# Values of the dilated heads: projected from neighbouring tokens, put in strided order through DRAM

## The chip, the cores and the metric

The kernel runs on one core of one Trainium2 chip. The metric is the device time of one execution in microseconds; lower is better. A core has TensorE (PE, with its weight loads shown apart as PEld), VectorE (DVE), ScalarE (ACT), GpSimd (POOL) and SyncE (SP), whose queue issues most of the DMAs here. Each engine works through its own instructions in program order.

## What is computed

Two layers of a hybrid decoder, for 512 prompt tokens and 64 sample tokens (8 sequences of 8) with shared weights. Only the attention of the prompt matters for this change:

```python
h = rmsnorm(x, norm1)
q, k, v, u, ga, gb = jnp.split(h @ w_in, ...)        # 12 heads of 64, in three groups of four
for g, (w, d) in enumerate(((128, 1), (512, 4), (2048, 16))):
    idx = q_idx[:, None] - jnp.arange(w // d + 1)[None, :] * d     # keys at distance 0, d, 2d, ...
    o[g], lse[g] = softmax attention of q over k[idx], v[idx]
o = sum over g of softmax(lse)[g] * o[g]
```

Queries of the two dilated groups meet only keys and values whose token number is the same modulo 4 (or 16). The keys and values are also outputs, in token order: the cache buffers of each group.

## The kernel before

Activations lie with the 1024 features on partitions: `h[k]` is one of eight tiles of 128 features by 576 tokens, split in a rounded part and a remainder (`h[k][:, 0]`, `h[k][:, 1]`). Weights stream in pieces of 512 KB (`raw`, two buffers, issued on SP's queue); ACT rounds each into `wh`, DVE subtracts to get `wl`, and each product is three matmuls (rounded by rounded, remainder by rounded, rounded by remainder).

A layer begins with nine units of the query, key and value projection: `UNITS = ("d", "a", "b", "e", "c")` for head pair p = 0, and the same without e for p = 1. Unit d makes query and key of group 0, a the queries and b the keys of groups 1 and 2, e the values of group 0 (both pairs), c the values of groups 1 and 2. In `qkv` (L450) a unit has two halves of one weight piece each; a half runs over four feature tiles k and four blocks j of 128 tokens, and each (k, j) is three matmuls of line L464 whose stationary operand is a 128 by 128 piece of `h[k]` and whose moving operand is 256 columns of weights, into the PSUM tile `mmq`. After each half eight matmuls of L476 do the sample tokens (`psd`). In all units but c, block j is the 128 neighbouring tokens 128j to 128j+127. In unit c, block j is every fourth token starting with j:

```python
def cls(v, r):
    return v[:, r:NP:4]
```

so that the values come out of the projection in the order in which the dilated heads use them.

`unit_out` (L482) takes a unit out of PSUM: four ACT operations multiply by the reciprocal root mean square of each token, a column of `rn` for each block. `stats` (L283) makes those columns: four for blocks of neighbouring tokens, one for the sample tokens, and four more (L292) for the blocks of every fourth token, which only unit c uses. It runs once a layer inside the first unit. For units d, a and b there follow a rotation on DVE (`rope`), transposes on PE (`trq`, L523) and the tiles `Td`, `Ta`, `Tb`; for c, the tile `vc`. Keys and values are written out by DMAs on SP's queue (L539 to L547).

`prompt(p)` (L549) is the attention of a head pair: scores (`sp`, L569 and L572), masks and maxima on DVE, exponentials on ACT, a mixing of the groups' weights by two small groups of matmuls (`ex`, L601 and L623), then `O`: eight steps, each of which scales a tile `P` on DVE (L639, L641), transposes it on PE (`trx`, L648) and multiplies by `ve` and `vc` (L661, L665). `decode(p, qb)` is the attention of the sample tokens over the caches: POOL multiplies cache pieces `kc` with the queries `qb` (`prod`), DVE sums the products (`SC<-prod`), later PE forms the outputs (`po`). The cache pieces and `qb` are DMAs on SP's queue; `qb` is itself spread through DRAM (`DQ`, `DR`).

The order of everything beside the main loops is fixed when the program is built, by a planner with a clock of its own, `now`. A main loop calls `tick(cost)` after each group (1.28 for the 12 matmuls of one k in `qkv`, whatever the unit; 0.72 for the six of one k in `gemm`). Side tasks are generators that sleep for some time, until an event (`mark`, with a delay `lat`), or until the planner's idea of an engine's end (`after`); whichever is due at a tick issues its next instructions there. `until` lets the planner's clock run on without main work. So planned times decide the order in each engine's queue, and the chip decides the rest. `prompt(p)` waits for the event `("V", "c", p)` just before it sets up `O`.

After the nine units come four groups of `u`, 16 gates with their products, `wo` and the feed-forward part, all `gemm` (L222, matmuls at L228). `until("S", 1)`, `until("ob", 0, l)` and `until("D", 1)` tie them to the attention.

The functions that the diff touches:

Of the kernel before, what the change touches and what calls it, by code (L numbers as in the profile page):

```python
# [7 lines left out]
F32 = mybir.dt.float32  # L8
F32R = mybir.dt.float32r
BF16 = mybir.dt.bfloat16  # L10
AF = mybir.ActivationFunctionType
# [26 lines left out]
def hybrid_decoder_kernel(ctx: ExitStack, tc: tile.TileContext, a, o):  # L38
    nc = tc.nc
    T, V, S, G, Q = nc.tensor, nc.vector, nc.scalar, nc.gpsimd, nc.sync  # L40
# [10 lines left out]
    drp = ctx.enter_context(tc.tile_pool(name="dr", bufs=1, space=DRAM))  # L51
# [15 lines left out]
    ident, ones, mask = C("ident"), C("ones"), C("mask")  # L67
# [90 lines left out]
    def mark(*key, lat=0.0):  # L158
        ev[key] = now[0] + lat
# [49 lines left out]
    V = Lane(V, 0.07, 960.0)  # L209
    S = Lane(S, 0.19, 1400.0)  # L210
    G = Lane(G, 0.1, 460.0)

    def post(delay, fn):
        def g():
            fn()
            return
            yield
        side(g(), delay)
# [49 lines left out]
    def cls(v, r):  # L268
        return v[:, r:NP:4]
# [11 lines left out]
        V.tensor_mul(r, r, q)  # L281

    def stats(sqs, full, key):  # L283
        n = 9 if full else 5
        ps = spp.tile([128, 512], F32, tag="s", name="st")
        for b in range(4):
            T.matmul(ps[:, b:b + 1], sqs[:, 128 * b:128 * b + 128], ones[:, 0:1], start=True, stop=True)
        for i in range(2):
            T.matmul(ps[64 * i:64 * i + 64, 4:5], sqs[:, NP:NT], ones[:, 0:1], start=True, stop=True)
        if full:  # L290
            for r in range(4):
                T.matmul(ps[:, 5 + r:6 + r], cls(sqs, r), ones[:, 0:1], start=True, stop=True)  # L292
        spend(0.2 * n)
        rs = tp.tile([128, 4, 9], F32, tag="rs", name="rs", bufs=2)
        rsqrt(rs, ps, n)
        r = rs[:, 2, :n]
        rb = tp.tile([128, NT], F32, tag="rb", name="rb", bufs=1)
        scale_of[key] = (rs[:, 2], rb)
        if full:
            mark("R", key, lat=max(V.t - now[0], 0.0) + 1.0)  # L300
        dgt = tp.tile([128, NT], F32, tag="t", name="dg")
        for b in range(5):
            m = 128 if b < 4 else 64
            dg = dgt[:, 128 * b:128 * b + m]
            V.tensor_scalar(out=dg[:m, :m], in0=ident[:m, :m], scalar1=r[:m, b:b + 1], scalar2=None, op0=ALU.mult)
        yield after(V, S, lag=1.6)
        ps2 = trp.tile([128, 512], F32, tag="tr", name="rps")
        for b in range(5):
            m = 128 if b < 4 else 64
            dst = ps2[:, 128 * b:128 * b + 128] if b < 4 else ps[:, 64:128]  # L310
            T.matmul(dst, ones[:m, :], dgt[:m, 128 * b:128 * b + m], start=True, stop=True)
        spend(1.0)
        S.copy(rb[:, 0:512], ps2)
        S.copy(rb[:, 512:576], ps[:, 64:128])
        if not full:
            mark("R", key)
# [41 lines left out]
    h, sqs = None, None  # L358
    for l in range(L):
# [90 lines left out]
        def qkv(p, unit):  # L450
            psm = mmp.tile([128, 4, 256], F32, tag="mm", name="mmq")
            psd = None
            for half in range(2):
                w = wnext()
                for kk in range(4):
                    k = 4 * half + kk
                    hi, lo = (w[i][:, 256 * kk:256 * kk + 256] for i in range(2))
                    for j in range(4):
                        if unit != "c":
                            xh, xl = (h[k][:, i, 128 * j:128 * j + 128] for i in range(2))  # L460
                        else:
                            xh, xl = (cls(h[k][:, i], j) for i in range(2))
                        for i, (x, ww) in enumerate(((xh, hi), (xl, hi), (xh, lo))):
                            T.matmul(psm[:, j], x, ww, start=(k == 0 and i == 0 and j % 2 == 0),  # L464
                                     stop=(k == 7 and i == 2 and j % 2 == 1), skip_group_check=True)
                    tick(1.28)
                if psd is None:
                    if (p, unit) != (0, "d"):
                        until("psd")
                        del ev[("psd",)]  # L470
                    psd = pdp.tile([128, 512], F32, tag="d", name="psd")
                for kk in range(4):
                    k = 4 * half + kk
                    hi, lo = (w[i][:, 256 * kk:256 * kk + 256] for i in range(2))
                    for i, ww in enumerate((hi, lo)):
                        T.matmul(psd[:, 0:256], hd[:, k], ww,  # L476
                                 start=(k == 0 and i == 0), stop=(k == 7 and i == 1))
                tick(0.85)
            side(unit_out(p, unit, psm, psd), ("R", ("a", l)))
            tick()  # L480

        def unit_out(p, unit, psm, psd):  # L482
            rn = scale_of["a", l][0]
            if unit == "e":
                nat = ve
            elif unit == "c":
                nat = pp.tile([128, 4, 256], F32, tag="vc", name="vc", bufs=1)
            else:
                nat = qp.tile([128, 4, 256], F32, tag="nat", name="nat", bufs=2)
            col = 0 if unit != "c" else 5  # L490
            for j in range(4):
                S.activation(nat[:, j], psm[:, j], AF.Copy, scale=rn[:, col + j:col + j + 1])
            dt = tp.tile([64, 256], F32, tag="t", name="dt")
            S.activation(dt, psd[64:128, 0:256], AF.Copy, scale=rn[64:128, 4:5])
            if unit == "d":
                dns[p] = dp.tile([64, 9, 128], F32, tag="dn", name="dn", bufs=1)
            DN = dns[p]

            def dsum(dst, c0, c1):
                src = psd[0:64, c0:c1]  # L500
                t = dt[:, c0:c1]
                if c1 - c0 == 256:
                    src, t = v3(src, 2), v3(t, 2)
                V.scalar_tensor_tensor(out=dst, in0=src, scalar=rn[0:64, 4:5], in1=t, op0=ALU.mult, op1=ALU.add)

            yield after(S)
            if unit == "e":
                dsum(DN[:, 6], 0, 128)
                dsum(ve1, 128, 256)
            else:  # L510
                dsum({"d": DN[:, 0:6:3], "a": DN[:, 1:3], "b": DN[:, 4:6], "c": DN[:, 7:9]}[unit], 0, 256)
            mark("psd")
            f0 = 128 * p
            if unit in "dab":
                if unit == "b":
                    side(decode_q(p, DN), 0.6)
                rope(nat.rearrange("p n (h d) -> p n h d", h=4), *rope_t, 128, 4, 4)
                yield after(V)
                tt = qp.tile([128, 2, 512], F32, tag="T" + unit, name="T" + unit, bufs=1)
                for i in range(2):  # L520
                    pt = trp.tile([128, 512], F32, tag="tr", name="trq")
                    for j in range(4):
                        T.transpose(pt[:, 128 * j:128 * j + 128], nat[:, j, 128 * i:128 * i + 128], ident)  # L523
                    spend(0.43)
                    dst = tt[:, i]
                    if unit != "d":
                        dst = dst.rearrange("p (r n) -> p n r", r=4)
                        pt = pt.rearrange("p (n r) -> p n r", r=4)
                    S.activation(dst, pt, AF.Copy, scale=0.125 if unit == "a" or (unit == "d" and i == 0) else 1.0)
                    yield 1.1  # L530
                tts[p][unit] = tt
                mark("T", unit, p, lat=0.3)
            else:
                if unit == "c":
                    vcs[p] = nat
                    side(decode_new(p, DN), 0.5)
                mark("V", unit, p, lat=0.3)
            if unit == "d":
                Q.dma_start(o["p128"][l, :, 0, f0:f0 + 128], nat[:, 3, 128:256])  # L539
            elif unit == "e":  # L540
                Q.dma_start(o["p128"][l, :, 1, :], nat[:, 3, :])
            elif unit in "bc":
                s = 0 if unit == "b" else 1
                order = "(b p) s f -> p b s f" if s == 0 else "(p b) s f -> p b s f"
                for i, n in enumerate(("512", "2048")):
                    Q.dma_start(o["p" + n][l].rearrange(order, b=4)[:, :, s, f0:f0 + 128],
                                nat[:, :, 128 * i:128 * i + 128])  # L547

        def prompt(p):  # L549
# [632 lines left out]
        h = hn  # L1182
# [127 lines left out]
```

## Time and profile before

| what | us |
|---|---|
| median of 3 runs | 1780.98 |
| the runs | 1780.54, 1780.98, 1784.67 |
| span of the profiled execution, first to last instruction | 1781.5 |
| PE busy in it | 1711.1 |
| DVE busy | 947.6 |
| ACT busy | 554.3 |
| POOL busy | 442.8 |

The profiled execution is told by its span; nothing else of its time is shown. The span stands 0.5 us above the median of the runs, so times read in the trace can be set against the median as they are. Layer 0 begins at 0 and layer 1 at about 884 us.

### The profile page before, as it was taken

How to read it: one execution, taken by the hardware profiler on the slowest of the kernel's cores; microseconds unless marked ns; L12 is line 12 of the kernel's file. 1: busy time of each engine (PE TensorE's matmuls, PEld its weight loads, DVE VectorE, ACT ScalarE, POOL GpSimd, SP SyncE). 2: the span in 40 equal slices, each digit the busy share in tenths (PEclk: the TensorE clock that was granted, in tenths of full speed). 3: DMA queues.
4: the chain of work that ended last, by engine and by line, in shares of the span. 5: the costliest groups of instructions: out<-in, count | busy, mean ns of one | idle time of the engine just before them, and what ended most of it. 6: DMA issues, size and time to landing. Idle time of an engine off the chain costs nothing. (4 is left out here: it accounts for less than half of the span.)

```text
span 1781.5 us, 30883 instructions
## 1 busy us (share of the span) xinstructions
PE 1711.1 (96%) x13008; PEld 1667.6 (94%) x13008; DVE 947.6 (53%) x1365; ACT 554.3 (31%) x882; POOL 442.8 (25%) x461
## 2 busy tenths in 40 slices
PE   8988999999999999999999799989999999999996
PEld 7978988989999999999999698888999999999996
DVE  6388679735544333343535977894454443434332
ACT  4423332223333222231334233311333331322232
POOL 2065128311111211211102622572111112121201
PEclk8999999999999999999999999999999999999998
DMA  4451653434244445443326326435243544444421
GB/s 157 156 164 62 197 155 116 130 105 144 99 166 165 173 156 175 153 176 117 120 89 202 105 97 209 134 99 168 68 158 120 173 168 165 156 174 155 172 84 54
DMA packets 137316, 251.04 MB, mean 141 GB/s; under 512 B 9532, under 2 KB 98108, under 8 KB 134346
## 3 DMA queue, kind: packets, MB, share of 16 engines
q1 hardware_dynamic: 132810, 194.27, 33.7%
q0 software_dynamic: 3648, 53.98, 8.4%
q8 instruction: 103, 1.69, 0.4%
q10 hardware_dynamic: 720, 0.82, 0.1%
q14 instruction: 35, 0.29, 0.1%
HBM read 237.30 MB, written 72.77 MB: 174 GB/s over the span
## 5 line engine op out<-in xcount | busy, mean ns | idle before, releaser
L228 PE MATMUL mm<-a,wh 128*128 128x256 f32 (+1 forms) x2304 | 413.2, 302 | 14.5 <-DVE mB L203 8.7
L203 DVE TENSOR_TENSOR wl<-raw,wh 128x1024 fp32r<-128x1024 f32 (+2 forms) x248 | 340.9, 1375 | 113.3 <-ACT wh L203 103.6
L228 PEld LDWEIGHTS mm<-a,wh 128*128 128x128 f32 x2304 | 350.5, 193 | 22.5 <-issue 21.5
L203 ACT CAST wh<-raw 128x1024 fp32r<-128x1024 f32 (+2 forms) x248 | 241.5, 974 | 403.7 <-PE mm L228 324.1
L228 PE MATMUL mm<-h,wh 128*128 128x256 f32 (+1 forms) x2048 | 354.8, 295 | 0.0
L228 PEld LDWEIGHTS mm<-h,wh 128*128 128x128 f32 x2048 | 306.2, 188 | 0.2
L203 POOL TENSOR_TENSOR prod<-kc,qb 128x1024 f32<-128x1024 f32 (+1 forms) x96 | 212.4, 2239 | 244.6 <-DMA kc<-in_c 191.8
L464 PE MATMUL mmq<-wh,a 128*128 128x256 f32 x1152 | 256.7, 318 | 3.1 <-DVE a L203 2.4
L228 PE MATMUL mm<-a,wl 128*128 128x256 f32 (+1 forms) x1152 | 249.4, 298 | 0.0
L464 PEld LDWEIGHTS mmq<-wh,a 128*128 128x128 f32 x1152 | 217.4, 228 | 6.3 <-DVE a L203 3.1
L228 PE MATMUL mm<-h,wl 128*128 128x256 f32 (+1 forms) x1024 | 218.0, 295 | 0.0
L203 POOL COPY pace<-beat 1x1 f32<-1x1 f32 x112 | 67.7, 605 | 544.9 <-DVE beat L203 544.9
L228 PE MATMUL mm<-m,wh 128*128 128x256 f32 (+1 forms) x1152 | 200.0, 295 | 0.0
L228 PEld LDWEIGHTS mm<-a,wl 128*128 128x128 f32 x1152 | 196.8, 192 | 0.0
L203 DVE TENSOR_TENSOR xr<-xr,mm 128x576 f32<-128x576 f32 (+2 forms) x88 | 61.6, 700 | 245.4 <-PE mm L228 221.9
L464 PE MATMUL mmq<-wl,a 128*128 128x256 f32 x576 | 181.0, 314 | 0.0
L228 PEld LDWEIGHTS mm<-m,wh 128*128 128x128 f32 x1152 | 173.3, 187 | 0.0
L228 PEld LDWEIGHTS mm<-h,wl 128*128 128x128 f32 x1024 | 171.4, 188 | 0.0
L464 PEld LDWEIGHTS mmq<-wl,a 128*128 128x128 f32 x576 | 131.4, 228 | 0.0
L203 ACT ACTIVATE zz<-z 128x576 f32<-128x576 f32 x64 | 43.9, 686 | 259.7 <-DVE z L203 259.7
L228 PE MATMUL mm<-m,wl 128*128 128x256 f32 x576 | 123.3, 295 | 0.0
L203 DVE SCALAR_TENSOR_TENSOR z<-mm,rb 128x576 f32<-128x576 f32 x64 | 48.5, 758 | 134.6 <-PE mm L228 128.0
(214 smaller groups left out, 1909.8 us busy)
## 6 DMA issues: line engine op xcount, KB each, us to landing
raw<-in_wup SPq DMA_DIRECT2D x64, 512.0 KB
raw<-in_wd SPq DMA_DIRECT2D x64, 512.0 KB
out_s<-in_c POOLq DMA_DIRECT2D x64, 508.0 KB, 3.9
kc<-in_c SPq DMA_DIRECT2D x40, 512.0 KB
raw<-in_wq SPq DMA_DIRECT2D x35, 512.0 KB
kc<-in_c SPq DMA_DIRECT2D x64, 256.0 KB
out_s<-in_c POOLq DMA_DIRECT2D x32, 504.0 KB, 4.8
raw<-in_wgb SPq DMA_DIRECT2D x16, 512.0 KB
```

Source lines behind the costliest of these rows:

```text
L203: return op(*args, **kw)
L228: T.matmul(ps[:, c0:c0 + t1 - t0], w, act[:, x, t0:t1], start=(i == 0 and j == 0), stop=(i == n - 1 and j == 2))
L464: T.matmul(psm[:, j], x, ww, start=(k == 0 and i == 0 and j % 2 == 0), stop=(k == 7 and i == 2 and j % 2 == 1), skip_group_check=True)
```

## The change

Unit c is projected like the other units, from blocks of 128 neighbouring tokens, with the columns of `rn` that the others use; the four extra columns of `stats` are gone. Its result goes to a tile `nat` (of the two buffers that d, a and b use in turn) and not to `vc`. From there a DMA writes it to a DRAM buffer `DV` in token order, and a second DMA reads `vc` from it so that block r holds every fourth token. Both are issued on SP's queue at planned times, 1.2 and 4.0 after the ACT operations. The event `("V", "c", p)` comes 9.0 after them on the planner's clock; it was 0.3 after the sums of the sample tokens. The cache outputs of unit c are now written from `nat` with the same row order as those of unit b.

```diff
     def stats(sqs, full, key):
-        n = 9 if full else 5
+        n = 5
...
-        if full:
-            for r in range(4):
-                T.matmul(ps[:, 5 + r:6 + r], cls(sqs, r), ones[:, 0:1], start=True, stop=True)
         spend(0.2 * n)
...
                     for j in range(4):
-                        if unit != "c":
-                            xh, xl = (h[k][:, i, 128 * j:128 * j + 128] for i in range(2))
-                        else:
-                            xh, xl = (cls(h[k][:, i], j) for i in range(2))
+                        xh, xl = (h[k][:, i, 128 * j:128 * j + 128] for i in range(2))
...
-            elif unit == "c":
-                nat = pp.tile([128, 4, 256], F32, tag="vc", name="vc", bufs=1)
             else:
                 nat = qp.tile([128, 4, 256], F32, tag="nat", name="nat", bufs=2)
-            col = 0 if unit != "c" else 5
             for j in range(4):
-                S.activation(nat[:, j], psm[:, j], AF.Copy, scale=rn[:, col + j:col + j + 1])
+                S.activation(nat[:, j], psm[:, j], AF.Copy, scale=rn[:, j:j + 1])
+            if unit == "c":
+                DV = drp.tile([512, 256], F32, tag=f"dv{l}{p}", name="DV")
+                vc = pp.tile([128, 4, 256], F32, tag="vc", name="vc", bufs=1)
+                vcs[p] = vc
+                post(1.2, lambda: Q.dma_start(DV.rearrange("(j p) f -> p j f", j=4), nat))
+                post(4.0, lambda: Q.dma_start(vc, DV.rearrange("(n r) f -> n r f", r=4)))
+                mark("V", unit, p, lat=9.0)
...
                 if unit == "c":
-                    vcs[p] = nat
                     side(decode_new(p, DN), 0.5)
-                mark("V", unit, p, lat=0.3)
+                else:
+                    mark("V", unit, p, lat=0.3)
...
-                order = "(b p) s f -> p b s f" if s == 0 else "(p b) s f -> p b s f"
                 for i, n in enumerate(("512", "2048")):
-                    Q.dma_start(o["p" + n][l].rearrange(order, b=4)[:, :, s, f0:f0 + 128],
+                    Q.dma_start(o["p" + n][l].rearrange("(b p) s f -> p b s f", b=4)[:, :, s, f0:f0 + 128],
                                 nat[:, :, 128 * i:128 * i + 128])
```

## Rows read from the trace of the kernel before

**Rows 1.** The page, part 1: busy us, share of the span, instructions.

```profile
PE 1711.1 (96%) x13008; PEld 1667.6 (94%) x13008; DVE 947.6 (53%) x1365; ACT 554.3 (31%) x882; POOL 442.8 (25%) x461
```

**Rows 2.** Busy us by stage: stretch, length, PE PEld DVE ACT POOL, clock, DMA, GB/s.

```profile
79.30:105.40 26.10, 26.10 (x132) 25.44 (x129) 15.56 (x20) 9.70 (x31) 9.83 (x5) 1.00 0.80 251
105.40:170.00 64.60, 50.41 (x416) 46.69 (x416) 61.33 (x67) 19.27 (x34) 42.99 (x19) 0.97 0.28 88
176.20:204.00 27.80, 27.80 (x150) 27.25 (x149) 12.19 (x26) 9.39 (x22) 0.00 (x0) 1.00 0.60 190
206.00:254.00 48.00, 46.76 (x457) 39.32 (x456) 37.48 (x83) 16.93 (x47) 11.17 (x22) 1.00 0.57 175
254.00:322.00 68.00, 60.19 (x429) 58.52 (x426) 62.85 (x61) 18.36 (x31) 53.41 (x24) 0.95 0.38 110
...
979.20:1042.00 62.80, 50.37 (x405) 46.73 (x405) 57.86 (x66) 17.71 (x33) 43.28 (x20) 0.95 0.30 94
```

**Rows 3.** The chain that ended last, layer 1: start, us, what.

```profile
1044.75 4.31 PE mmq L464 x36
...
1050.02 11.20 PE mmq L464 x48
...
1361.14 349.96 PE mm L228 x2634
```

**Rows 4.** PEld groups in 79.3 to 105.4, unit c: busy us, mean ns.

```profile
L464 PEld LDWEIGHTS mmq<-wh,a 128*128 128x128 f32 x64 | 17.9, 328 | 0.2
```

**Rows 5.** PEld groups in 57.5 to 69.0, units b and e.

```profile
L464 PEld LDWEIGHTS mmq<-wh,a 128*128 128x128 f32 x56 | 8.7, 190 | 0.0
```

**Rows 6.** Timeline of PE inside `stats`, layer 0: start, us, instruction.

```profile
31.21 0.95 PE L287 MATMUL st<-const,sqs 128*128 128x1 f32 x8
...
32.30 2.03 PE L292 MATMUL st<-const,sqs 128*128 128x1 f32 x8
```

**Rows 7.** Busy us behind `stats`, layer 0, columns as in the second group.

```profile
33.00:40.00 7.00, 7.00 (x41) 6.81 (x41) 3.73 (x16) 2.53 (x7) 0.00 (x0) 0.76 0.07 28
```

**Rows 8.** PE's waits in 105.4 to 170: us in total, times, longest.

```profile
PE trx L648 <- DVE P L203: 7.3, 7, 1.6
PE trq L523 <- DVE nat L203: 4.9, 2, 3.5
PE ex L623 <- DVE xt L203: 2.0, 1, 2.0
```

**Rows 9.** Groups in 105.4 to 170: busy us, mean ns, idle before.

```profile
L203 POOL TENSOR_TENSOR prod<-kc,qb 128x1024 f32<-128x1024 f32 (+1 forms) x19 | 43.0, 2284 | 18.8 <-DVE SC L203 15.7 <-DVE cc L203 3.1
...
L203 DVE TENSOR_REDUCE SC<-prod 128x16 f32<-128x1024 f32 (+1 forms) x22 | 21.7, 1013 | 0.0
L203 DVE TENSOR_SCALAR P<-P,cc 128x256 f32<-128x256 f32 (+1 forms) x16 | 18.6, 1199 | 0.0
```

**Rows 10.** DVE groups in 226 to 249, the same step of p = 1.

```profile
L203 DVE TENSOR_SCALAR P<-P,cc 128x256 f32<-128x256 f32 (+1 forms) x16 | 4.7, 343 | 0.0
```

**Rows 11.** Timeline of POOL: the first products of `decode(0)`.

```profile
92.48 6.09 POOL L203 TENSOR_TENSOR prod<-kc,qb 128x1024 f32<-128x1024 f32 x3 [75.47 <-DMA kc<-in_c]
100.87 3.77 POOL L203 TENSOR_TENSOR prod<-kc,qb 128x512 f32<-128x512 f32 x2 [2.29 <-DMA kc<-in_c]
```

**Rows 12.** Timeline of DVE at the end of unit c, p = 0.

```profile
106.40 0.17 DVE L203 COPY ct<-ex 128x16 f32<-128x16 f32 x1 [4.28 <-PE ex L601]
```

**Rows 13.** Timeline of PE: `O` set up, then its first use of `vc`.

```profile
113.40 0.38 PE L632 MATMUL O<-zero 1*128 1x512 bf16 x1
...
122.34 0.61 PE L665 MATMUL O<-PT,vc 128*64 128x128 f32 x8
```

**Rows 14.** Waits of SP's queue, whole span: us in total, times, longest.

```profile
SPq L111 <- DVE wl L203: 1201.2, 235, 12.3
...
SPq L695 <- DMA DR<-DQ: 17.8, 2, 9.0
...
SPq L707 <- DMA DS<-dn: 10.5, 4, 4.1
```

**Rows 15.** Waits of all engines: what the pooling mixer's tiles waited for.

```profile
POOL u L203 <- DMA out_p<-vc: 45.2, 1, 45.2
```

## The prediction

> **What bounds the kernel now.** I read the page first: PE is busy 96% of the span, the next engine 53% [rows 1]. So PE's own work sets the time, unless a stage says otherwise. Then I cut the first layer into stages [rows 2]. In the stretch 79.30 to 105.40, which is unit c of p = 0, PE is never idle. In the next, 105.40 to 170.00, PE is idle 14.2 us (64.60 less 50.41) and DVE is busy 61.33: this stage is DVE's. Unit c of p = 1 (176.20 to 204.00) is again all PE, 206 to 254 nearly so (1.2 idle), and 254 to 322 is DVE's once more (62.85 of 68). Layer 1 repeats it; its row for the first of DVE's stages has 12.4 idle. After the attention one unbroken run of PE matmuls of 350 us is on the chain that ended last [rows 3], so a gain that has reached that point lasts to the end. What is to be seen: PE time saved in unit c is worth its full size only where PE sets the next handover. The p = 1 unit leads into PE's stage, the p = 0 unit into one of DVE's.
>
> **The projection in unit c.** The chain holds the last 36 matmuls before unit c and 48 of unit c in one piece each [rows 3]: 4.31/36 = 0.1197 us against 11.20/48 = 0.2333 us, with the same operand sizes. The weight loads tell where it goes: 328 ns each in unit c [rows 4], 190 ns in the units before it [rows 5], at the full clock. The one thing that differs is the fourfold step of the loaded columns. Unit c has 96 matmuls of L464, so it saves 96 x 0.1136 = 10.9 us; two pairs and two layers make 43.6.
>
> **The statistics.** The four strided columns are eight matmuls that took 2.03 us where the eight unstrided ones took 0.95 [rows 6]. They begin 1.9 us before the next work does, so 1.9 goes per layer, 3.8 in all. That the step alone doubles a load shows here in another kind of matmul. Behind them, in layer 0, the granted clock was 0.76 over 7 us [rows 7]: about half of it at 1.2 instead of 2.4 GHz, worth 7 x 0.24 = 1.7 us. A shorter run of one-column matmuls may keep the clock up; I take 0, with 0 to 1.7 for the range. On the other side more PE idle in DVE's stage may lower it there: its rows stand at 0.97 and 0.95 already, and 0.03 of 64.6 is 1.9 per layer for one more fall; I take 0 here too.
>
> So PE has 47.4 us less to do. How much arrives?
>
> **p = 0, into DVE's stage.** PE reaches the first group of mixing matmuls (`ex`, end of unit c) at 79.3 - 1.9 + 26.1 - 10.9 = 92.6 instead of 105.4. Before, DVE sat 4.28 us until 106.40 for it [rows 12]. But POOL's first product started at 92.48, after its cache piece had landed [rows 11], and that piece hangs on unit b, which moves by 1.9 alone: 90.6. The sum of the first product stands on DVE ahead of what `ex` needs, so `ex` can't run before about 90.6 + 2.3 + 1.0 + 0.6 = 94.5. Two of the 12.8 us are lost at once. Then DVE has only sums to do until `O` is set up: POOL feeds a product each 2.28 us, a sum takes 1.01 [rows 9]. `O` is now held by the planner for 9.0 of its units after unit c; at 1.28 for a k that PE does in 12 x 0.12 = 1.44 us, with 0.85 and 0.8 of other work and the wait of 2.0 that `ex` had before [rows 8], about 12.4 us behind unit c's end at 96.6: 109. It stood at 113.40 [rows 13], so the eight scaling steps, which with the sums fill DVE, start 4.4 us earlier. In the wait DVE does one or two sums that it did later before, worth 1.5. I take 6 us saved per layer. The bounds are 0 (the stage ends when it did) and 12.8 (all of it).
>
> **p = 1, into PE's stage.** Unit c is 27.8 us with DVE busy 12.2 of it [rows 2]; after, 16.9 with the same 12.2, that is 72%. The rotation, transposes and scores of that unit still fit, more tightly. I take 10 of 10.9; the low bound is half, 5.5, if the denser order makes PE wait for the scores' DVE work. The stages behind it begin with what PE hands over, and move along whole.
>
> **The trip through DRAM.** Per unit c two DMAs of 512 KB on SP's queue. No row of before shows these; the nearest are waits of SP for a write to DRAM that is read back: up to 4.1 us for 192 KB and up to 9.0 us for 1.5 MB [rows 14]. Each leg between these, with 1.9 us of ACT before them, puts `vc` in place 10.1 to 19.9 us after unit c's end. In p = 0 the first use of `vc` came 8.9 us after `O` was set up [rows 13], so it would now come at 12.4 + 8.9 = 21.3: hidden at both ends, margin 1.4 at the worse. In p = 1 the scaling steps begin not before 226 [rows 10], 22 us after unit c's end, before any use of `vc`. Cost taken: 0. The bytes are 4 MB in 1781 us. Without that cover, each us late stops PE a us at `O`.
>
> What the read stops behind it is SP's queue: it waits there for the write, and weight pieces and cache pieces stand behind. SP's weight pieces waited for DVE 235 times, 5.1 us on average [rows 14]: they are issued when a buffer comes free, two to three pieces ahead of their use, so a hold of 4.1 to 9.0 us, partly within such a wait, should not reach PE. The Trainium skill, DMA: Bandwidth & Descriptors, section Rules for kernel authors, speaks against the change: a DMA that reads what another wrote has to wait at its issuer for the first one's completion. The trace agrees by those 9.0 and 4.1 us; by that rule, if every hold of 9.0 came through to PE, the sum would be 36 us worse, and by the rows' slack nothing worse.
>
> Small things at 0: ACT's operations are as many as before; the buffers of `nat` come round after two units of some 13 us, later than the worst 9.0 of a DMA; the reciprocal roots of five columns for nine hide on DVE. The pooling mixer's tiles waited for cache outputs of `vc` once [rows 15]; if they take the place of `nat`, one more DMA is ahead of them: 0 to 4.1 us per layer, taken as 0 since DVE's scores come first.
>
> **The sum:** 2 x (6 + 10) = 32 us of 1781.5. The span stands 0.5 above the median, so I write 1749.
>
> **Rivals.** *DVE's stage keeps its end* (p = 0 gives nothing). For it: POOL waited 15.7 us there for DVE's sums, and DVE's scaling takes 1199 ns beside POOL's products and 343 ns without them [rows 9, 10], so the two engines take turns, whatever PE does; and the planner holds `O` back. Against it: the turn-taking starts earlier, as worked out. Time: 1781 - 20 = 1761. The Trainium skill, SBUF — State Buffer, section Who interferes with whom, says that such a VectorE operation and a GpSimd one that reads SBUF block each other wholly through a shared port. By that rule, too, the stage lasts as long as its products do; the trace agrees with 1199 against 343 ns.
>
> *All of it arrives.* For it: with more sums done before the scaling starts, fewer products are left beside it, and PE meets the stage further on in its own work. Against it: the first product's start. Time: 1781 - 47 = 1734.
>
> *`vc` comes late, or SP's hold shows.* For it: margin 1.4 us in p = 0 at the worse end, and SP may first wait up to 12.3 us for DVE [rows 14]; `vc` then lands 1.9 + 9.0 + 12.3 + 9.0 = 32.2 us after unit c, 10.9 past its use. Against it: such a wait delays DVE's scaling too. Time: 1749 + 2 x 10.9 = 1771.
>
> *Slower:* the same hold, on weight pieces or in both pairs. The saving of 16 per layer is gone when `vc` of p = 0 lands 16 us past its use, 37 us after unit c's end; at 45 us it would be 1749 + 2 x 24 = 1797. It takes two waits of SP like the longest in the trace in one chain, which no row shows.
>
> *The loads don't get faster* because something else in unit c slows them: only DVE's load and the DMAs differ, and the strided columns of `stats` were slow without either. Then 1781 - 4 = 1777, about the same.
>
> **How the numbers follow.** My forecast, 1741 to 1757 by its own terms, has 0.50; DVE's stage keeping its end 0.20; all arriving 0.14; `vc` late 0.10; the loads unchanged 0.03; slower 0.03. The range 1735 to 1765 leaves out half of the case in which all arrives and most of the last three. A measurement of this kernel tells about 0.3%, 5 us, from no change: faster 0.94, same 0.03, slower 0.03.
>
> **What would show it.** Right: weight loads of L464 near 190 ns throughout, no L292, unit c near 15 us of PE, the `ex` matmuls waiting for DVE, the p = 0 stage with some 20 us of PE idle, the p = 1 stages moved along whole. Wrong: PE waiting for a DMA at L665, weight pieces late behind SP's read of `DV`, or unit c still at 0.23 us a matmul. The weakest number is the 6 us.

## The result and the profile after

The changed kernel took 1771.32 us (median of five runs, 1767.13 to 1774.63) beside 1784.67 for the kernel before (1780.54 to 1787.21): a ratio of 0.9938, 95% interval 0.9918 to 0.9958 (the two medians alone give 0.9925). It is faster by 0.6% where 1.8% was forecast, and 1771 lies above the range of 1735 to 1765. The profiled execution has a span of 1769.3 us.

The page's busy times, after (PE: busy us, share of the span, instructions):

```profile
PE 1678.0 (95%) x12992; PEld 1632.7 (92%) x12992; DVE 941.1 (53%) x1365; ACT 553.6 (31%) x882; POOL 440.1 (25%) x461
```

Against [rows 1], PE is busy 33.1 us less, but it is idle 1769.3 - 1678.0 = 91.3 us where it was 1781.5 - 1711.1 = 70.4. So 33.1 us of work went, 20.9 us of idle time came, and 12.2 us are left. The question is where PE now waits.

Weight loads of unit c, p = 1, in 174 to 187 (busy us, mean ns), after:

```profile
L458 PEld LDWEIGHTS mmq<-wh,a 128*128 128x128 f32 x49 | 7.6, 189 | 0.1
```

The projection does what was forecast: 189 ns a load, as in the units beside it, where [rows 4] has 328. The stages, after, with the columns of [rows 2]:

```profile
33.00:40.00 7.00, 7.00 (x59) 6.81 (x58) 3.50 (x10) 3.99 (x9) 0.00 (x0) 1.00 0.09 9
74.66:96.73 22.07, 15.35 (x133) 14.49 (x129) 15.37 (x20) 9.70 (x31) 7.24 (x4) 0.94 0.78 242
96.73:116.69 19.96, 18.66 (x104) 18.23 (x105) 15.10 (x22) 4.36 (x8) 15.90 (x7) 0.63 0.68 209
172.00:187.30 15.30, 15.30 (x133) 14.86 (x133) 11.91 (x25) 6.43 (x14) 0.00 (x0) 1.00 0.49 151
200.00:220.00 20.00, 10.40 (x53) 9.90 (x52) 7.56 (x20) 1.77 (x5) 6.92 (x14) 0.67 0.60 201
```

Unit c of p = 0 is 15.35 us of PE followed by a wait of 6.7 for `ex`, and the 20 us behind that wait, up to the set-up of `O`, ran at a granted clock of 0.63. Unit c of p = 1 is 15.3 us without a gap. The wait is for DVE's two `xt` multiplications (DVE's timeline):

```profile
91.65 1.22 DVE L203 TENSOR_REDUCE SC<-prod 128x16 f32<-128x1024 f32 x1 [4.92 <-POOL prod L203]
92.79 3.79 DVE L203 TENSOR_TENSOR xt<-stt,const 128x32 f32<-128x32 f32 x2
```

ACT takes unit e out of PSUM, just where unit c of p = 0 begins, at 74.22 (78.85 before), unit b of p = 1 at 170.59 (175.55 before) and unit c of p = 1 at 187.32 (201.82 before). The gain is 4.6 us, then 5.0, then 14.5. Of the 4.6, 1.3 lie ahead of the statistics, which begin at 29.94 (31.21 before [rows 6]), and 3.4 come from the statistics themselves. So unit c of p = 1 gives what was forecast, and unit c of p = 0 next to nothing. This is the stretch from unit e to unit b of p = 1 in both layers, in the kernel before and then in the changed one:

```profile
78.85:175.55 96.70, 82.51 (x599) 78.08 (x596) 81.87 (x94) 30.92 (x69) 52.82 (x24) 0.98 0.42 133
953.15:1049.10 95.95, 83.52 (x599) 79.17 (x596) 80.38 (x94) 30.91 (x68) 52.79 (x24) 0.96 0.42 133
```

```profile
74.22:170.59 96.37, 79.81 (x599) 75.26 (x596) 80.09 (x94) 31.04 (x69) 51.18 (x24) 0.86 0.47 144
940.84:1037.39 96.55, 77.84 (x599) 73.45 (x596) 79.68 (x94) 31.03 (x67) 51.21 (x24) 0.89 0.46 145
```

It takes as long as before. PE is busy 2.7 and 5.7 us less in it, where unit c alone was to save 10.9, and the granted clock has fallen from 0.98 and 0.96 to 0.86 and 0.89.

The last row of the stages, 200 to 220, is new as well. Between 200 and 220 PE is busy 10.4 of 20 us, at a granted clock of 0.67: two thirds of the stretch at 1.2 GHz instead of 2.4. What it waits for, in the timelines of PE, DVE and SP's queue after (start, us, instruction, idle before and its releaser):

```profile
202.13 0.42 PE L228 MATMUL mm<-a,wl 128*128 128x256 f32 x2
210.71 1.65 PE L817 MATMUL po<-pb,kvn 128*128 128x128 f32 x6 [8.14 <-POOL pb L203]
```

```profile
198.03 0.79 DVE L203 TENSOR_REDUCE dsm<-SC 128x16 f32<-128x368 f32 x1
208.08 0.69 DVE L203 TENSOR_TENSOR u<-mm,rb 128x512 f32<-128x512 f32 x1 [9.26 <-DMA out_p<-nat]
208.69 0.21 DVE L203 TENSOR_TENSOR ud<-mm,rb 128x64 f32<-128x64 f32 x1
208.82 0.25 DVE L203 RECIPROCAL dsm<-po 128x16 f32<-128x16 f32 x1
209.10 0.54 DVE L203 TENSOR_TENSOR SC<-SC,dsm 128x368 f32<-128x368 f32 x1
```

```profile
183.60 6.66 SPq L725 DMA_DIRECT2D kc<-in_c  x1
190.36 3.70 SPq L728 DMA_DIRECT2D kc<-in_c  x2
194.16 0.74 SPq L725 DMA_DIRECT2D kc<-in_c  x1
195.00 1.63 SPq L692 DMA_DIRECT2D qb<-DR  x1
196.68 0.43 SPq L488 DMA_DIRECT2D DV<-nat  x1
197.16 2.36 SPq L543 DMA_DIRECT2D out_p<-nat  x2
```

Read backwards: PE waits 8.1 us for POOL's `pb`, which needs the `SC` that DVE writes at 209.10, and that stands on DVE behind `u`. DVE sat 9.26 us before `u`, until a cache output of `nat` had landed. ACT had filled `nat` by 187.32 + 1.53 = 188.9, but SP's queue was in the decode's cache loads and in `qb` until 196.6, and so issued the transfers that read `nat` 8 us later; they landed some 10 us after that. POOL waits there too: its clearing of `u`'s first columns, which stands ahead of `pb` in POOL's order, starts at 208.26. DVE's `u` came at 214.61 before, so of the 14.5 us there are 6.5 left. From ACT's activations of unit c to `u` it is 20.8 and 21.5 us in the two layers, and it was 12.8 in both: 8.0 and 8.7 us are lost. In layer 1 the chain that ended last runs through the same place (start, us, what):

```profile
1050.85 5.83 SPq L725
1056.78 3.60 SPq L728
...
1063.92 0.94 SPq L488
1064.91 0.50 SPq L543
1065.46 10.05 DMA out_p<-nat
1075.63 0.69 DVE u L203
```

What joins `u` and `nat` would be memory: `nat` lies in the pool that is closed before the tiles `u` are opened, and these take its place. In the kernel before, unit c's result lay in `vc`, in another pool, and only the earlier `nat` of unit b was in the way. That was the theory to test.

### The profile page after: what moved, and what is told of

It is laid out like the page before. It is cut to its first block, busy times and chain, and to the rows that moved or that the text cites. A ratio compares the mean times of both kernels' runs of the same rounds, so it can differ in the third digit from the quotient of the medians.

```text
span 1769.3 us, 30870 instructions
## 1 busy us (share of the span) xinstructions
PE 1678.0 (95%) x12992; PEld 1632.7 (92%) x12992; DVE 941.1 (53%) x1365; ACT 553.6 (31%) x882; POOL 440.1 (25%) x461
## 5 line engine op out<-in xcount | busy, mean ns | idle before, releaser
L203 DVE TENSOR_TENSOR wl<-raw,wh 128x1024 fp32r<-128x1024 f32 (+2 forms) x248 | 330.6, 1334 | 110.1 <-ACT wh L203 100.3
L458 PE MATMUL mmq<-wh,a 128*128 128x256 f32 x1152 | 225.1, 295 | 3.2 <-DVE a L203 3.0
L458 PEld LDWEIGHTS mmq<-wh,a 128*128 128x128 f32 x1152 | 187.4, 199 | 6.9 <-DVE a L203 3.8
L458 PE MATMUL mmq<-wl,a 128*128 128x256 f32 x576 | 167.4, 291 | 0.0
L458 PEld LDWEIGHTS mmq<-wl,a 128*128 128x128 f32 x576 | 114.6, 199 | 0.0
```

The lines of the kernel that those rows point to most:

```text
L203: return op(*args, **kw)
```

## Experiments

Ratios are to the kernel before, run on the same chip; its medians there were 1780.42, 1780.66 and 1785.16 us in the three groups below.

**The memory.** Three runs, with a fourth on the due time.

```diff
# own_buffer
+            elif unit == "c":
+                nat = dp.tile([128, 4, 256], F32, tag="vn", name="vn", bufs=1)
...
-            ve1 = dp.tile([64, 128], F32, name="ve1")
+            ve1 = ud.rearrange("p g t -> p (g t)")[0:64, 0:128]
```

> Unit c's natural-order result gets a 4 KB tile of its own in the decode pool, outside the memory that the pooling mixer's tiles u take over (a 0.5 KB scratch is moved to make room); everything else, the round trip too, stays as in the changed kernel. Theory A (the loss is u waiting until the transfers that read unit c's result in the reused memory have landed): DVE's two waits of 9.3 and 10.0 us for out_p<-nat before u go, u starts near 200 in layer 0 instead of 208.1, and the time falls by about 2 x 8 us to 1755 (1748 to 1762). Theory B (the round trip's own traffic and its place in SP's queue are the loss, wherever the result lies): stays at 1767 to 1775. Theory C (DVE's and POOL's own order of work is the bound there, the wait only fills a gap): the waits go but PE waits as long for POOL's pb, 1764 to 1772.

```diff
# act_queue
-                post(1.2, lambda: Q.dma_start(DV.rearrange("(j p) f -> p j f", j=4), nat))
+                S.dma_start(DV.rearrange("(j p) f -> p j f", j=4), nat)
+                for i, n in enumerate(("512", "2048")):
+                    S.dma_start(o["p" + n][l].rearrange("(b p) s f -> p b s f", b=4)[:, :, 1, 128 * p:128 * p + 128],
+                                nat[:, :, 128 * i:128 * i + 128])
...
-            elif unit in "bc":
-                s = 0 if unit == "b" else 1
+            elif unit == "b":
+                s = 0
```

> Unit c's result stays in the reused memory, but the three transfers that read it (the write to DRAM and the two cache outputs) are issued on ScalarE's queue right behind the four activations that fill it, instead of behind the decode loads in SP's queue. Theory A: they land some 10 us earlier, u starts near 200 in layer 0, 1755 (1749 to 1764; ScalarE pays about 3 us a unit for the issues). Theory B (traffic): 1767 to 1775, as the same bytes move. Theory C: 1764 to 1772 with PE waiting for pb as before.

```diff
# no_trip
+            elif unit == "c":
+                nat = pp.tile([128, 4, 256], F32, tag="vc", name="vc", bufs=1)
...
-                DV = drp.tile([512, 256], F32, tag=f"dv{l}{p}", name="DV")
-                vc = pp.tile([128, 4, 256], F32, tag="vc", name="vc", bufs=1)
-                vcs[p] = vc
-                post(1.2, lambda: Q.dma_start(DV.rearrange("(j p) f -> p j f", j=4), nat))
-                post(4.0, lambda: Q.dma_start(vc, DV.rearrange("(n r) f -> n r f", r=4)))
+                vcs[p] = nat
```

> Block loads and five statistics columns as in the changed kernel, but no round trip: the activations write unit c's values straight into the tile that the attention reads, in token order, so the dilated heads take their values from the wrong tokens. The planner's due time of 9.0 us is kept. Theory A: 1753 (1746 to 1760), the same as with a buffer of its own within 4 us, since the trip itself hides. Theory B: also about 1753, but with a buffer of its own it is 1767 or more, so that the two runs lie over 10 us apart. Theory C: 1764 to 1772 here too.

```diff
# no_trip_soon, on top of no_trip
-                mark("V", unit, p, lat=9.0)
+                mark("V", unit, p, lat=0.3)
```

> As the run without the round trip (values in token order, so the dilated heads read wrong tokens), and the planner's due time of the values is set back from 9.0 to 0.3 us, as in the kernel before. If the planner's hold keeps the set-up of O late in head pair 0 (116.7 us in the changed kernel, 109 forecast), O comes 3 to 8 us earlier and the time is 3 to 10 us under the run with 9.0; if O is held by the second exchange and the DVE's chain behind it, the two runs agree within 2 us.

| run | us | ratio, 95% interval |
|---|---|---|
| own_buffer | 1751.60 | 0.9837 (0.9816 to 0.9858) |
| act_queue | 1749.11 | 0.9825 (0.9804 to 0.9846) |
| no_trip | 1746.74 | 0.9804 (0.9785 to 0.9822) |
| no_trip_soon | 1742.43 | 0.9777 (0.9756 to 0.9798) |

Two different edits, one that moves the bytes elsewhere and one that reads them sooner, give the same 18 to 20 us (0.9938 less 0.9837 or 0.9825, of 1780). Theory A said 1755 and holds; B and C said 1764 or more for both and fall. From ACT's activations of unit c to `u` it is now 11.4 us with a buffer of its own and 12.7 on ScalarE's queue, in both layers. Not all of the 18 to 20 us is this wait: the stretch from unit e to unit b of p = 1 takes 92.67 and 94.73 us with the buffer and 93.75 and 93.85 with the queue, 2 to 4 less than in the changed kernel, and some of it is lost again behind `u`. With a buffer of its own, the cache outputs are still issued late on SP's queue, and DVE no longer cares; SP's queue and DVE there:

```profile
193.09 0.43 SPq L490 DMA_DIRECT2D DV<-vn  x1
193.57 1.61 SPq L545 DMA_DIRECT2D out_p<-vn  x2
```

```profile
194.10 0.79 DVE L203 TENSOR_REDUCE dsm<-SC 128x16 f32<-128x368 f32 x1
194.81 0.69 DVE L203 TENSOR_TENSOR u<-mm,rb 128x512 f32<-128x512 f32 x1
```

DVE writes `u` while SP is still issuing the output of the tile: no wait. On ScalarE's queue the reads of `nat` go out right behind the activations, and are done when DVE comes to `u` (ACT, then DVE):

```profile
184.60 1.54 ACT L203 ACTIVATE nat<-mmq,rs 128x256 f32<-128x256 f32 x4
186.16 0.37 ACTq L488 DMA_DIRECT2D DV<-nat  x1
186.57 1.50 ACTq L490 DMA_DIRECT2D out_p<-nat  x2
```

```profile
196.58 0.75 DVE L203 TENSOR_REDUCE dsm<-SC 128x16 f32<-128x368 f32 x1
197.26 0.67 DVE L203 TENSOR_TENSOR u<-mm,rb 128x512 f32<-128x512 f32 x1
```

PE's idle time in the run with its own buffer is 1751.2 - 1678.1 = 73.1 us at the same busy time as in the changed kernel: the whole difference of 18.2 us is idle time that has gone. What the trip itself costs is small: without it the time is 2.4 to 4.9 us lower, and the intervals overlap (Theory A had own_buffer and no_trip within 4 us, and they are 4.9 apart). The earlier due time gives 4.3 more without the trip, at intervals that overlap too, while its runs spread from 1739 to 1751; O came at 108.3 us instead of 115.4, as that theory said, but what this is worth the run doesn't tell.

**The other terms.** Four runs: the statistics alone, and three that start from act_queue.

```diff
# stats_alone, on the kernel before
-        n = 9 if full else 5
+        n = 5
...
-        if full:
-            for r in range(4):
-                T.matmul(ps[:, 5 + r:6 + r], cls(sqs, r), ones[:, 0:1], start=True, stop=True)
...
-            col = 0 if unit != "c" else 5
+            col = 0
```

> The kernel before, strided loads kept, with the statistics cut from nine columns to five; unit c's activations then scale with the block columns, so the dilated values are scaled wrongly. The prediction's term: 1.9 us a layer on TensorE, 3.8 in all, so 1776 to 1778 beside 1780 and shorter stats stretches. Rival: the stretch waits for DVE's rsqrt chain and not for the columns, 0 to 1 us.

```diff
# weigh_act
-                V.tensor_scalar(out=pj[:, c0:256], in0=pj[:, c0:256], scalar1=cc[:, 5, j, hh:hh + 1], scalar2=None,
-                                op0=ALU.mult)
-                V.tensor_scalar(out=pj[:, 256:], in0=pj[:, 256:], scalar1=cc[:, 2, j, hh:hh + 1], scalar2=None,
-                                op0=ALU.mult)
+                S.activation(pj[:, c0:256], pj[:, c0:256], AF.Copy, scale=cc[:, 5, j, hh:hh + 1])
+                S.activation(pj[:, 256:], pj[:, 256:], AF.Copy, scale=cc[:, 2, j, hh:hh + 1])
...
             weigh(*steps[0])
-            yield after(V)
+            yield after(V, S)
```

> As the run with the transfers on ScalarE's queue, and the 16 scalings of P in each unit of the prompt's attention run as activations on ScalarE (17.6 us busy in the 65 us from 105 to 170) instead of on DVE (57.7 busy there). If DVE taking turns with POOL is what took most of head pair 0's gain (6 of 12.8 us forecast to arrive), each layer gains 3 to 6 us: 1738 to 1744. If TensorE is held there by the products on POOL and the second exchange, P's scaling only moves: 1746 to 1752.

```diff
# v_due_3
-                mark("V", unit, p, lat=9.0)
+                mark("V", unit, p, lat=3.0)
```

> As the run with the transfers on ScalarE's queue, with the due time of the re-read values set from 9.0 to 3.0 us. Set-up of O, 114.0 us in layer 0 there, comes at 108 to 110. If the trip is back in time (the read of vc was issued at 108.5 us, its data some 4 us later), 1743 to 1747, as without the trip; if TensorE comes to the first product of the dilated values before they have landed, it waits in order and the gain is lost: 1748 to 1755, with a wait for vc in the trace.

```diff
# pool_later
-            yield (6.0, 0.5)[p]
+            yield (18.0, 0.5)[p]
```

> As the run with the transfers on ScalarE's queue, but head pair 0's decode products on POOL start 12 us of planned time later, so that they do not run beside DVE's first exchange. If POOL's products slow DVE there (the two xt multiplications took 3.8 us in the changed kernel), xt takes under 1 us, DVE's wait before it (4.1 us) goes and the first exchange comes 3 to 6 us earlier; the time moves to 1744 to 1747 if that exchange sets the stage's end, and rises to 1752 to 1760 if the products themselves do.

| run | us | ratio, 95% interval |
|---|---|---|
| stats_alone | 1774.67 | 0.9958 (0.9942 to 0.9973) |
| weigh_act | 1737.62 | 0.9749 (0.9727 to 0.9772) |
| v_due_3 | 1752.95 | 0.9840 (0.9816 to 0.9864) |
| pool_later | 1766.94 | 0.9922 (0.9899 to 0.9945) |

*stats_alone* gained 7.5 us by its ratio (4.8 to 10.3; the two medians differ by 6.0), more than the term of 3.8, so the rival of 0 to 1 falls. The stretch behind the statistics, 33 to 40, in this run:

```profile
33.00:40.00 7.00, 7.00 (x59) 6.81 (x58) 2.86 (x6) 3.18 (x6) 0.00 (x0) 1.00 0.22 61
```

The granted clock is 1.00 where it was 0.76 [rows 7]: the 1.7 us that the prediction bounded and then set to 0. With it the term is 5.5, inside the interval. The traces agree: from the statistics to ACT's activations of unit e layer 0 takes 47.64 us in the kernel before and 44.29 in this run, layer 1 takes 59.57 and 57.71, together 5.2.

*pool_later* takes POOL's products away from the first exchange. Its two `xt` multiplications on DVE, and those of act_queue, in 80 to 170 (busy us, mean ns), each from its own trace:

```profile
L203 DVE TENSOR_TENSOR xt<-stt,const 128x32 f32<-128x32 f32 x2 | 0.3, 191 | 0.0
```

```profile
L203 DVE TENSOR_TENSOR xt<-stt,const 128x32 f32<-128x32 f32 x2 | 2.4, 1238 | 0.0
```

Alone on DVE they take 191 ns each, beside POOL's products 1238. PE ran `ex` at 89.71 us there, without a wait, 4.7 earlier than in act_queue (94.40), and the stretch from unit e to unit b of p = 1 takes 87.84 and 88.69 us in the two layers, where act_queue has 93.75 and 93.85. So the exchange beside the products did hold this stage. The run is 18 us slower than act_queue all the same, outside what was expected of it: the loss lies behind the stage, where layer 0 takes 689.4 us from `u` to the next layer's statistics and act_queue 676.0. POOL's products, in pool_later and in act_queue (ns min/median/max, first and last start us):

```profile
L203 POOL TENSOR_TENSOR prod<-kc,qb x24: 1260/2434/3338, 89.3 to 162.9; 128x1024 f32<-128x1024 f32 x16, 128x512 f32<-128x512 f32 x8
```

```profile
L203 POOL TENSOR_TENSOR prod<-kc,qb x24: 1264/2405/3721, 88.3 to 151.9; 128x1024 f32<-128x1024 f32 x16, 128x512 f32<-128x512 f32 x8
```

The last product starts 11 us later, and what hangs on it later too; which wait brings the loss no run here shows. In *v_due_3* O was set up at 108.8, PE waited for `vc` 0.5 us in layer 1 and not at all in layer 0, and the time did not fall (1753): both of its theories missed. The scalings that came earlier ran beside the products, whose last start moved from 151.9 to 157.3; `xt` took 3.8 us in this run and 2.4 in act_queue, so the two effects aren't told apart. *weigh_act* takes the scalings off DVE, and the last product starts at 149.5. The stretch from unit e to unit b of p = 1 takes 88.05 and 86.81 us, 6 to 7 less than in act_queue, and the time, 1737.6, lies at the edge of what the first theory had (1738 to 1744). The scalings in 105 to 170 there, and in 200 to 240, the same step of p = 1:

```profile
L203 ACT ACTIVATE P<-P,cc 128x256 f32<-128x256 f32 (+1 forms) x16 | 6.9, 488 | 0.0
```

```profile
L203 ACT ACTIVATE P<-P,cc 128x256 f32<-128x256 f32 (+1 forms) x16 | 7.0, 497 | 0.0
```

On ACT one takes 488 ns beside the products and 497 without them, where DVE needs 1199 and 343 [rows 9, 10]. The Trainium skill, SBUF — State Buffer, section Who interferes with whom, has VectorE and GpSimd sharing a port pair that one holds against the other, and ScalarE with ports of its own. The traces agree: 191 against 1238 ns on DVE, and 497 against 488 ns on ACT.

**The best version, and what belongs to the change.** Three runs.

```diff
# weigh_act_due_3: weigh_act with
-                mark("V", unit, p, lat=9.0)
+                mark("V", unit, p, lat=3.0)
# before_weigh_act: the kernel before with the edit of weigh_act
# before_again: the kernel before, unchanged
```

> The two last edits together: transfers on ScalarE's queue, P scaled on ScalarE, due time of the re-read values 3.0 us. With DVE relieved, the scalings of P can follow the earlier set-up of O at once: if so, 2 to 5 us under the 1738 of the run with 9.0 (1732 to 1737). If unit d's and a's TensorE work already covers the hold, or POOL's products set the stage's end, the same within 2 us: 1736 to 1740.

> The kernel before (strided loads, nine statistics columns, no round trip) with P scaled on ScalarE instead of DVE. If DVE was a bound beside TensorE there already, it gains about as much as on the changed kernel (11.5 us): 1767 to 1771. If TensorE's strided loads set the pace and DVE only became the bound once they had gone, 0 to 6 us: 1774 to 1781.

> The kernel before once more, for a second profile of its statistics stretch. If the low granted clock behind the statistics (0.79 from 34 to 42 us) belongs to the nine columns, it is there again; if it was chance, the stretch is at 1.00 here.

weigh_act_due_3 took 1739.49 us, ratio 0.9745 (0.9721 to 0.9768): the same as weigh_act. O comes at 105.8 there, and now PE does meet the trip (PE's waits in 90 to 170, us, times, longest):

```profile
PE O L663 <- DMA vc<-DV: 2.9, 1, 2.9
```

before_weigh_act took 1768.16, ratio 0.9916 (0.9891 to 0.9942), 15 us under the kernel before. The scaling on ScalarE is thus worth about as much without the change (15) as with it (0.9825 less 0.9749, 13.5 us): DVE was a bound of its own in the kernel before already. The stretch from unit e to unit b of p = 1 takes 87.63 and 87.65 us there, with the strided loads, as long as in weigh_act without them: the loads do not set its length. Of weigh_act's 2.5% about 1.75 belong to the change with its reads on ScalarE's queue. before_again, one run of 1785.43, had the low clock behind the statistics again:

```profile
33.00:40.00 7.00, 7.00 (x45) 6.81 (x45) 3.73 (x16) 3.16 (x9) 0.00 (x0) 0.76 0.00 1
```

In layer 1 the first 14 to 16 us from the same statistics on ran at 0.89 in this run and at 1.00 in the kernel before, so the nine columns alone do not settle it.

## Why the prediction was wrong, step by step

**The step that failed** is the one on the pooling mixer's tiles: "if they take the place of `nat`, one more DMA is ahead of them: 0 to 4.1 us per layer, taken as 0 since DVE's scores come first". It measured 9.3 and 10.0 us of DVE's time, and 8.0 and 8.7 us of each layer's gain went with it. The place was right and three things in it were not. The bound of 4.1 was SP's wait for one write; here 8 us of SP's queue stand ahead of the transfers, because the issues of the cache loads, planned earlier, come first, and the landing took 10. DVE's scores do come first, but they end at 198.8, 9.3 us before `u` can start. And the cost was taken to fall on `u` alone, while `SC`, which PE's next work needs by way of POOL, stands behind `u` in DVE's order. The row that the step quotes [rows 15] does not show such a wait for certain: POOL's clearing of `u` began 0.46 us after ACT's activation of `SC` there, and in layer 1 0.51 after it, where the profile names ACT and not a transfer. The range ended at 1765, and this term at its upper bound would have given 1757; the bound was too low by more than half.

**A second step, p = 0, failed with it.** "I take 6 us saved per layer": 1.9 of the 6 are the statistics, and about 4 were to come from unit c. The stretch from unit e to unit b of p = 1 got 0.3 us shorter in layer 0 and 0.6 longer in layer 1; against the other profiles with strided loads, before_again and stats_alone, where it takes 96.9 to 97.6, it is 1 us shorter at most. PE was ready for `ex` at 90.0 instead of 105.4. But `xt`, 0.6 us at most in the sum (its two multiplications took 178 ns each in the kernel before), took 3.8 beside POOL's products, so `ex` came at 96.73 (bound given: 94.5). Behind this wait PE ran at a clock of 0.63 up to `O`, at 116.69 (forecast: 109), later than before [rows 13].

**The rest of the sum.** With the wait for the memory taken out the time is 1749 to 1752, 29 to 31 us under its own kernel before, where 32 was forecast. That the total comes so near is in part luck, as its terms do not:

- *The loads, 43.6 us of PE:* right in mechanism and size per load (189 ns). PE's busy time fell by 33.1 and not by the whole 47.4. Of the 14.3 that are missing 13.4 lie in the two p = 0 stretches, where it fell by 2.7 and 5.7 instead of 10.9 each, for the same 599 matmuls at a lower clock.
- *The statistics, 3.8:* mis-sized, 5.2 in the traces (4.8 to 10.3 by the run time), because the clock behind them in layer 0 was taken at 0.
- *p = 0, 6 of 12.8:* 3.7 and 1.3 in the changed kernel, statistics included. In own_buffer and act_queue, where `xt` takes 2.4 us and not 3.8, it is 3 to 7.
- *p = 1, 10 of 10.9:* right; 9.5 from unit b's ACT to unit c's, in both layers.
- *The trip, 0:* nearly right. PE never waited for `vc` in the changed kernel; the runs without the trip put at most 5 us on it.
- *The clock, 0:* wrong. In the p = 0 stretches it fell from 0.98 and 0.96 to 0.86 and 0.89.

Of the rivals, "`vc` comes late" gives 1771, the measured time, by a mechanism that did not happen: no engine waited for `vc`. "DVE's stage keeps its end" is what p = 0 did in the changed kernel. It gives 1761, so without the wait for the memory it does not explain the time either.

## What to carry to other kernels

When a result moves to another pool, list who takes that memory next and who reads it last: the wait falls on the taker, and it ends when the last read has landed, which counts from the place of that read in its queue and not from the moment at which the data are ready. Then look at what stands behind the taker on its own engine; here one `u` held back a small reduction that PE needed. A gain that grows as forecast up to one handover and shrinks there points to a new wait, and PE's idle time, beside its busy time, says so on the page at once. To see what one stage gained, take its length between the same two instructions in both traces.

## What was not expected of the hardware

- Two tiny DVE multiplications (128 by 32) took 178 to 191 ns each alone and 1238 to 1935 beside POOL's products; ACT did the scalings of `P` at 488 ns each beside the products and at 497 without them.
- Behind nine statistics columns the granted clock was 0.76 over 7 us of layer 0 in both profiles of the kernel before, behind five 1.00 in the changed kernel and in stats_alone. PE was busy all 7.00 us in each of these rows; what came ahead of the fall were eight strided one-column matmuls in 2.03 us [rows 6]. That stretch ran about half at 1.2 GHz. In layer 1 the stretch from the same columns on ran at 0.89 in one of the two profiles and at 1.00 in the other.
- A cache output of 256 KB landed 10.05 us after its issue in layer 1, in a stretch (1054.12 to 1075.63) where the DMA engines were busy 0.93 of the time.
